# Encoder layer: two PSUM banks for attention's results and two for its scores, later v transposes, other homes, later sigmoids

## The chip, the cores and the metric

The kernel runs on one core of a Trainium2 chip. The core has a matrix engine, TensorE (PE), whose weight loads are listed apart (PEld); a vector engine, VectorE (DVE); a scalar engine, ScalarE (ACT); GpSimd (POOL); and SyncE (SP), which in this kernel issues nearly all transfers. Each engine takes its own instructions in order, and semaphores tie the engines together. PE writes into PSUM, which has eight banks of 128 x 512 float32 numbers; the other data lie in SBUF. The metric is the device time of one execution in microseconds (us), median of several. Lower is better.

## What is computed

One layer of an encoder on a sequence of 2048 tokens of width 1024, in float32:

```python
h = rms_norm(x, norm_mix[l])
z = h @ w_in[l]
q_a, k_a, v_a, q_b, k_b, v_b, g_a, g_b = jnp.split(z, offsets, axis=-1)
y_a = windowed_gqa(q_a, k_a, v_a, sink[l])           # 8 heads, 2 kv heads, |t-s| <= 128, ALiBi, sink
y_b = neighborhood_attn(q_b, k_b, v_b, rpb[l])       # 8 heads, 8 x 16 neighbourhood on a 32 x 64 grid
gates = jax.nn.sigmoid(jnp.concatenate([g_a, g_b], axis=-1) + b_gate[l])
merged = (gates[..., :D_MODEL] * (y_a @ w_proj_a[l])
          + gates[..., D_MODEL:] * (y_b @ w_proj_b[l]))
x = x + merged @ w_out[l]
h2 = rms_norm(x, norm_mlp[l])
x = x + jnp.square(jax.nn.relu(h2 @ w_up[l])) @ w_down[l]
return rms_norm(x, norm_final)
```

## The kernel before

Float32 products are made of three matmuls on split operands: each operand is cast to a high part (ACT) and the rest is kept as a low part (DVE or POOL), and high x high, high x low and low x high are added up in one PSUM bank (`mm3`, L202 to L205). One such triple over one of the eight slices of 128 features is called a plain step here; eight make a tile of 128 features by 512 tokens (`feature_steps`, L214).

The tokens are handled in four blocks of 512. An opening stage normalises `x` and makes `z` for blocks 0 and 1. Then comes the stretch that the change touches. In it PE does three things in turn: the plain steps of `z` for blocks 2 and 3 (the generator `fill`, a chain of tiles in the list `dense`), attention A (32 units: 2 kv heads by 16 query blocks, class `Unit`) and then attention B (32 units: 8 heads by 4 column groups, class `Near`). After it follow the gate stage (`gated`, L1474), the up and the down projection.

The order of PE in this stretch is written out by hand. `issued[0]` is the last PE instruction of the order, and `in_turn()` (L781) queues what is traced inside it behind that instruction. It binds only instructions on the same engine. All else (ACT, DVE, POOL, SP) is ordered by a scheduler, which places what its own simulation holds to be ready first, earlier lines of the program first.

A unit of A makes four scores (`score`, L801; matmuls L816): each takes an `s` bank, and DVE (L820) adds the bias, writes the sum to SBUF and takes the maximum. After the fourth, ACT makes the exponentials (L827) and POOL scales them (L831). Then, for each of up to three chunks of 128 keys, `turn` (L834) transposes the four parts into a `pt` bank (L838), ACT casts them to `ph` (L842), DVE makes `pl` (L843), and `product` (L846) multiplies them with the values into an `av` bank (L853, L854). After the last chunk ACT and DVE take the result out of that bank (L860, L861) and it is stored (`put`, and L176 a unit later). B does the same with four pairs of chunks to a unit (L1037 scores, L1044 DVE, L1052 exponentials, L1057 POOL, L1068 transposes, L1075 and L1076 parts, L1089 products, L1097 and L1098 result).

Scores of A run three units ahead of the products (`AHEAD`), those of B two units. The table `FIRST` (L907) says how many plain steps are given before certain scores of the first three units of A; scores before the first entry are not bound to the order. In the loops (L940, L1116) a turn is followed by scores of a later unit, then by plain steps up to a share of the whole (`plain`, L917), then by the product of the chunk before.

Tiles of v need a transpose by PE: `v_tile` (L728) copies the finished tile to SBUF (`A.copy(vt, ps)`, L737) and yields "turn"; the next call of `plain` then runs on to `v_parts` (L420), whose four transposes (L423) take another `mm` bank, and whose result ACT and DVE split (L436, L437) and SP stores (L741).

PSUM is shared out as `mm` 2 banks, `s` 3, `pt` 2, `av` 1 (L685). A request for a bank gets one that is free, and its first matmul waits for the readers of its old content.

SBUF is filled from two sides by pools (L691, L692 for A, L968, L969 for B). Pools of B lie where pools of A lay, so the first write to a tile of B waits for the last use of what lay there. Of the ones that matter, `qb2` (queries of every third unit of B) lies over the end of A's `pl`, `braw1` over the end of `ph`, and `biasl` (the wide biases, made by POOL from `braw` and `masks`, L994) over the rest of `ph` and the start of `pl`; `qb1` lies over `biasa1` and `byhead`. Units of B load their queries and make their bias in `load` (L1014; the loads are L988 and L1017).

At the end, `last_exp` (L1052) holds the last exponential of B, and the sigmoids of the gate stage (L1486) are queued behind it on ACT. The products of the second half of the gates take the three `s` banks (L1479).

Of the kernel before, what the change touches and what calls it, by code (L numbers as in the profile page):

```python
# [8 lines left out]
F32 = mybir.dt.float32  # L9
F32R = mybir.dt.float32r  # L10
# [12 lines left out]
P = 128  # L23
KC = D // P
NB = 4
BT = 512
# [69 lines left out]
def encoder_layer(ctx, tc, x, norm_mix, w_in, b_gate, sink, rpb, w_pa, w_pb, w_out,  # L96
# [112 lines left out]
        for _ in feature_steps(ps, hl, pages):  # L209
            pass  # L210

    issued = [None]

    def feature_steps(ps, hl, pages):  # L214

        hi, lo = pages
        for k in range(KC):
            issued[0] = mm3(ps, hl[:, 0, k, :], hl[:, 1, k, :], hi[k // 4][:, k % 4, :], lo[k // 4][:, k % 4, :],
                            k == 0, k == KC - 1)
            if k < KC - 1:  # L220
                yield "step"

# [459 lines left out]


    s_pp = ExitStack()
    pps.update({t: pool(f"pp_{t}", space=PSUM, stack=s_pp) for t in ("mm", "s", "pt", "av")})  # L685
    s_w = ExitStack()
    wp = pools(s_w, "right", ("raw", "whl", "z"), "w")
    s_h = ExitStack()
# [39 lines left out]
    def v_tile(col):  # L728
        raw = load_slice([(cols(w_in[0], col), KC)])
        yield  # L730
        hl = split_slice(raw, V if col == O_VA else G)
        yield
        for b in (2, 3):
            ps = psum("mm", 2)
            yield from feature_steps(ps, hl, hp[b])
            vt = T(wp, [P, 2, BT], F32, "z", 3)[:, 0]
            A.copy(vt, ps)  # L737
            yield "turn"
            out = v_parts(col, b, vt, psum("mm", 2), T(wp, [P, 2, BT], F32, "z", 3).rearrange("p a b -> p (a b)"))
            for dst, t in out:  # L740
                SY.dma_start(dst, t)  # L741
            yield


# [39 lines left out]
    class Unit:  # L784
# [16 lines left out]
        def score(self, u, forced=True):  # L801
            g, s = self.g, self.s
            if u == 0:
                if bias_a[g] is None:
                    with tc.issue_after(shares[2]):
                        make_bias_a(g)
                self.st = T(ap_, [P, 8, 4], F32, "sta", 8)
            mx, nm, sm, es, ri = (self.st[:, k, :] for k in range(5))
            sink_g = sink_p[:, g : g + 1]
            lo, hi = self.span[u]  # L810
            n = hi - lo
            base = (self.i - 1) * P
            ps = psum("s", 3)
            with in_turn() if forced else nullcontext():
                for z in range(2):
                    ins = PE.matmul(ps[:, :n], self.q[:, u].rearrange("p h q -> p (h q)"), kas[g][:, z, base + lo : base + hi],  # L816
                                    start=z == 0, stop=z == 1).ins
            if forced:
                issued[0] = ins
            V.tensor_tensor_reduce(out=s[:, u, lo:hi], in0=ps[:, :n], in1=bias_a[g][:, lo - u * A_Q : hi - u * A_Q],  # L820
                                   scale=1.0, scalar=sink_g, op0=ALU.add, op1=ALU.max, accum_out=mx[:, u : u + 1])
            if u < 3:
                return
            A.activation(nm, mx, AF.Copy, scale=-1.0)
            A.activation(es, mx, AF.Exp, bias=sink_g, scale=-1.0)
            for u, (lo, hi) in enumerate(self.span):
                A.activation(s[:, u, lo:hi], s[:, u, lo:hi], AF.Exp, bias=nm[:, u : u + 1], accum_out=sm[:, u : u + 1])  # L827
            V.tensor_tensor(out=sm, in0=sm, in1=es, op=ALU.add)
            V.reciprocal(ri, sm)
            for u, (lo, hi) in enumerate(self.span):  # L830
                share = G.tensor_scalar(s[:, u, lo:hi], s[:, u, lo:hi], ri[:, u : u + 1], 1.0, ALU.mult, ALU.mult)  # L831
            shares.append(share.ins)

        def turn(self, c):  # L834
            pt = psum("pt", 2)
            with in_turn():
                for u in range(4):
                    ins = PE.transpose(pt[:, u * P : (u + 1) * P], self.s[:, u, c * P : (c + 1) * P], ident).ins  # L838
            issued[0] = ins
            ph = T(ap_, [P, 512], F32R, "ph", 3)  # L840
            pl = T(ap_, [P, 512], F32R, "pl", 3)
            A.copy(ph, pt)  # L842
            V.tensor_tensor(out=pl, in0=pt, in1=ph.bitcast(F32), op=ALU.subtract)  # L843
            return ph, pl

        def product(self, c, ph, pl):  # L846
            g, i, c0, c1 = self.g, self.i, self.c0, self.c1
            v = vas[g]
            if c == c0:
                self.po = psum("av", 1)  # L850
            po = self.po
            with in_turn():
                PE.matmul(po, v[:, i - 1 + c, :], ph, start=c == c0, stop=False)  # L853
# [50 lines left out]
        load_kv(g, 0)  # L904
    units = [Unit(g, i) for g in (1, 0) for i in range(7)] + [Unit(g, i) for g in range(2) for i in range(7, 16)]
    AHEAD, PLAIN, SCORE, STEP = 3, 24 * KC, 0.27, 0.68
    FIRST = {(0, 3): 12, (1, 2): 14, (2, 0): 16, (2, 2): 18, (3, 0): 21}  # L907

    def prepare(n):
        if n + 2 < len(units):  # L910
# [1 line left out]
        if n + 1 < len(units):  # L912
            units[n + 1].order()

    given, owed = 0, [False]

    def plain(upto):  # L917
        nonlocal given
        while given < upto:
            if owed[0]:  # L920
                with in_turn():
                    next(fill)
            with in_turn():
                owed[0] = next(fill) == "turn"
            given += 1

    units[0].load()
# [2 lines left out]
    for n in range(AHEAD):  # L930
        prepare(n)
        for u in range(4):
            if (n, u) in FIRST:
                plain(FIRST[n, u])
            units[n].score(u, (n, u) >= (0, 3))
    plain(FIRST[AHEAD, 0])
    chunks = [(n, c) for n, x in enumerate(units) for c in range(x.c0, x.c1)]
    behind, scored, begin = [], 0, given
# [18 lines left out]
            y.product(*z)  # L957
    y, *z = behind.pop(0)
    y.product(*z)
    if owed[0]:  # L960
        next(fill)
        owed[0] = False
    flush(queue=SY)
    s_a.close()


    s_b = ExitStack()
    bp = pools(s_b, "right", ("masks", "kb0", "qb0", "braw0", "biass0", "stb", "biass1", "qb1", "qb2", "biasl", "braw1", "kb1"), "b")  # L968
    bp.update(pools(s_b, "left", ("sb0", "sb1", "sb2", "vb0", "vb1", "vb2", "phb", "plb", "yb"), "b"))  # L969
    boff, bstart, btotal = bias_layout()  # L970
    last_exp, last_parts, n_raw, n_short = [None], [None], [0], [0]
# [36 lines left out]
    class Near:  # L1008
# [17 lines left out]
        def score(self, i, forced=True):  # L1026
# [4 lines left out]
            kv = self.k.rearrange("p z (q f) -> p z q f", q=8)  # L1031
            s = self.s
            n = B_NR[i] * w
            ps = psum("s", 3)
            with in_turn() if forced else nullcontext():
                for z in range(2):
                    ins = PE.matmul(ps[:, :n], self.q[:, i, :],  # L1037
# [42 lines left out]
        def product(self, pair, ph, pl, pieces):  # L1080
            kp = 4 * self.w
            if pair == 0:
                self.po = psum("av", 1)
                pieces.reverse()
            po = self.po
            with in_turn():
# [29 lines left out]
    for at, (n, p) in enumerate(pairs):  # L1116
        x = units[n]
        if p == 0:
            if n % 4 == 2 and n + 6 < len(units):
                kbs[(n + 6) // 4] = load_k((n + 6) // 4)  # L1120
            if n + 3 < len(units):
                bias = units[n + 3].load(bias)
        if p == 1 and n + 2 < len(units):
            units[n + 2].load_v()
        behind.append((x, p, *x.turn(p)))
        if n + 2 < len(units):
            units[n + 2].score(p)
            scored += 1
        plain(begin + round(((at + 1) / len(pairs) * whole - scored * SCORE) / STEP))
        if len(behind) > 1:  # L1130
            y, *z = behind.pop(0)
            y.product(*z)
    y, *z = behind.pop(0)
    y.product(*z)
    flush(queue=SY)
    s_b.close()
    s_pg = ExitStack()
# [48 lines left out]
        def tile(self, *a, **k):  # L1186
            return psum("av", 1)

    wo = []

    def load_wo(n):
        rv = T(p4x, [P, D], F32, "xr", 5)
# [275 lines left out]
    for b in range(NB):  # L1468
# [5 lines left out]
        def gated(f, n):  # L1474
# [1 line left out]
            if n == 0:  # L1476
                hls[f] = slice_of([(cols(w_pa[0], f * P), 4), (cols(w_pb[0], f * P), 4)], V)
            hl = hls[f]
            ps = psum("mm" if n == 0 else "s", 2 if n == 0 else 3)  # L1479
            for c in range(4):  # L1480
                mm3(ps, hl[:, 0, 4 * n + c, :], hl[:, 1, 4 * n + c, :], yh[n][:, c], yl[n][:, c], c == 0, c == 3)
            if (b, f, n) not in loaded_gates:
# [284 lines left out]
```

## Time and profile before

| | us |
|---|---|
| median of 3 runs | 2614.03 (2612.89 to 2614.96) |
| the profiled execution | 2616.45 |
| its span, first to last instruction | 2614.0 |

The granted TensorE clock of the execution was 0.997 on the mean. Busy time by stage, in us, from the profile's windows:

| window | what runs | PE | DVE | ACT | POOL |
|---|---|---|---|---|---|
| 360 to 380 | first scores of A | 18.29 | 6.96 | 7.72 | 5.38 |
| 600 to 640 | end of A, start of B | 35.28 | 18.41 | 20.01 | 20.45 |
| 640 to 760 | B | 118.16 | 60.79 | 69.38 | 61.35 |
| 760 to 1020 | B | 256.40 | 112.24 | 143.42 | 119.43 |
| 1020 to 1040 | last plain steps | 20.00 | 7.09 | 8.53 | 0.00 |

How to read rows: in a timeline, a row is start, duration, engine, line of the kernel, operation, tiles out<-in, shape, count of merged instructions, and in brackets the idle time before it with the instruction or transfer that ended it. Matmuls overlap: a row's duration reaches into the next row. In the lists of waits a row is who waited for whom, microseconds in total, number of times, longest.

### The profile page before, as it was taken

The numbers are of one execution on the slowest core, as the hardware profiler recorded it, in microseconds if no ns is written. First come the engines' busy times: TensorE is split into PE (matmuls) and PEld (weight loads), VectorE is DVE, ScalarE is ACT, GpSimd is POOL, SyncE is SP. The second block draws the span as 40 slices with busy tenths as digits, with TensorE's granted clock in tenths as the row PEclk, the third lists the DMA queues.
The fourth block names the chain that finished last, engine by engine and source line by source line (L and its number), as shares of the span: only waits on it lengthen the run. The fifth ranks groups of instructions, "written<-read, shape, count | busy, mean of one in ns | idle before, by whom it ended". The sixth has DMA issues, their size and how long they took to land.

```text
span 2614.0 us, 34536 instructions
## 1 busy us (share of the span) xinstructions
PE 2571.5 (98%) x12140; PEld 2145.5 (82%) x12140; DVE 1608.9 (62%) x2621; ACT 1233.6 (47%) x2261; POOL 366.1 (14%) x493
## 2 busy tenths in 40 slices
PE   8999999999999999999999999999999999999999
PEld 6888878877888888888888888888888888888887
DVE  8866566665544443756578777766656535554766
ACT  5335356765555555533335544644444322322454
POOL 1000024444555541000001000100000000000010
PEclk9999999999999999999999999999999999999999
DMA  5657486566886746855556765854428835445555
GB/s 185 203 155 203 135 251 166 127 170 176 203 213 173 210 128 194 269 180 155 173 184 207 243 209 202 308 185 148 155 97 306 301 97 184 144 146 170 185 189 174
DMA packets 354125, 490.38 MB, mean 188 GB/s; under 512 B 28808, under 2 KB 188808, under 8 KB 351776
## 3 DMA queue, kind: packets, MB, share of 16 engines
q1 hardware_dynamic: 346896, 471.14, 58.3%
q10 hardware_dynamic: 7056, 17.04, 1.7%
q8 instruction: 95, 1.56, 0.3%
q14 instruction: 78, 0.64, 0.1%
HBM read 328.64 MB, written 159.45 MB: 187 GB/s over the span
## 4 chain that ended last, share of the span: by engine, by line
PE 90%; DMA 3%; DVE 3%; ACT 2%; issue 1%; SPq 1%; POOL 0%; POOLq 0%; DVEq 0%; ACTq 0%
PE b L311 15%; PE b L312 15%; PE b L313 15%; PE mm L203 5%; PE mm L205 5%; PE mm L204 5%; PE zb L311 3%; PE zb L313 3%; PE zb L312 3%; PE pt L203 2%; PE pt L204 2%; PE pt L205 2%; PE av L1089 2%; PE pt L1068 2%; PE s L1037 2%; PE pt L838 1%
## 5 line engine op out<-in xcount | busy, mean ns | idle before, releaser
L312 PE MATMUL b<-dwh,dah 128*128 128x512 f32 x896 | 348.5, 389 | 0.0
L313 PE MATMUL b<-dwh,dah 128*128 128x512 f32 x896 | 347.6, 389 | 0.0
L311 PE MATMUL b<-dwh,dah 128*128 128x512 f32 x896 | 339.6, 389 | 0.0
L307 ACT CAST dah<-da 128x1024 fp32r<-128x1024 f32 (+1 forms) x128 | 120.5, 942 | 369.2 <-PE b L313 245.3
L308 DVE TENSOR_TENSOR dah<-da,dah 128x1024 fp32r<-128x1024 f32 (+1 forms) x128 | 139.7, 1091 | 224.2 <-ACT dah L307 221.2
L312 PE MATMUL b<-ubh,uwhlb 128*128 128x512 f32 x592 | 230.4, 389 | 0.4 <-DVE ubh L308 0.4
L311 PE MATMUL b<-ubh,uwhlb 128*128 128x512 f32 x592 | 230.2, 389 | 0.0
L313 PE MATMUL b<-ubh,uwhlb 128*128 128x512 f32 x592 | 229.2, 389 | 0.0
L203 PE MATMUL mm<-hT,whl 128*128 128x512 f32 x544 | 219.5, 404 | 0.0
L205 PE MATMUL mm<-hT,whl 128*128 128x512 f32 x544 | 215.2, 396 | 0.0
L204 PE MATMUL mm<-hT,whl 128*128 128x512 f32 x544 | 214.6, 394 | 0.0
L313 PEld LDWEIGHTS b<-dwh,dah 128*128 128x128 f32 x896 | 168.2, 188 | 34.9
L311 PEld LDWEIGHTS b<-dwh,dah 128*128 128x128 f32 x896 | 168.2, 188 | 34.9
L312 PEld LDWEIGHTS b<-dwh,dah 128*128 128x128 f32 x896 | 168.2, 188 | 34.8
L311 PE MATMUL zb<-zh,zwhl 128*128 128x512 f32 x476 | 186.6, 394 | 6.6 <-DVE st L251 1.8
L312 PE MATMUL zb<-zh,zwhl 128*128 128x512 f32 x476 | 186.5, 392 | 0.0
L313 PE MATMUL zb<-zh,zwhl 128*128 128x512 f32 x476 | 183.6, 392 | 0.3 <-DVE zwhl L308 0.3
L302 DVE TENSOR_TENSOR uc<-b,uc 128x512 f32<-128x512 f32 x160 | 109.2, 689 | 104.1 <-PE b L313 103.1
L1637 POOL TENSOR_TENSOR st<-st,power 128x1 f32<-128x1 f32 x16 | 13.3, 841 | 925.2 <-DVE st L1636 925.2
L312 PEld LDWEIGHTS b<-ubh,uwhlb 128*128 128x128 f32 x592 | 111.2, 188 | 23.7 <-DVE ubh L308 0.8
L311 PEld LDWEIGHTS b<-ubh,uwhlb 128*128 128x128 f32 x592 | 111.1, 188 | 23.4 <-issue 0.4
L313 PEld LDWEIGHTS b<-ubh,uwhlb 128*128 128x128 f32 x592 | 111.1, 188 | 23.1
(255 smaller groups left out, 5847.4 us busy)
## 6 DMA issues: line engine op xcount, KB each, us to landing
at<-uc SPq DMA_DIRECT2D x224, 256.0 KB
da<-at SPq DMA_DIRECT2D x96, 512.0 KB
dw<-in_w_down_dram SPq DMA_DIRECT2D x160, 256.0 KB
uraw<-in_w_up_dram SPq DMA_DIRECT2D x32, 1024.0 KB
raw<-in_w_in_dram SPq DMA_DIRECT2D x34, 512.0 KB
zraw<-in_w_in_dram SPq DMA_DIRECT2D x16, 1024.0 KB
z<-zg SPq DMA_DIRECT2D x64, 256.0 KB
zg<-zc SPq DMA_DIRECT2D x32, 256.0 KB
```

The costliest lines, as they stand in the source:

```text
L203: PE.matmul(ps, lh, rh, start=first, stop=False)
L204: PE.matmul(ps, lh, rl, start=False, stop=False)
L205: return PE.matmul(ps, ll, rh, start=False, stop=last).ins
L302: return eng.tensor_tensor(out=out, in0=a, in1=b, op=op).ins
L307: casts.append(A.copy(hi, src).ins)
L308: return eng.tensor_tensor(out=lo, in0=src, in1=hi.bitcast(F32), op=ALU.subtract).ins
L311: PE.matmul(ps, lh, rh, start=first, stop=False, skip_group_check=True)
L312: PE.matmul(ps, lh, rl, start=False, stop=False, skip_group_check=True)
L313: PE.matmul(ps, ll, rh, start=False, stop=last, skip_group_check=True)
L1037: ins = PE.matmul(ps[:, :n], self.q[:, i, :], kv[:, z, B_R0[i] // 4 : (B_R0[i] + B_NR[i]) // 4, 4 * B_C0[j] : 4 * (B_C0[j] + w)], start=z ...
L1068: ins = PE.transpose(pt[:kp, at + (i - i0) * P : at + (i - i0 + 1) * P], self.s[i][:, rr : rr + kp], ident).ins
L1089: ins = PE.matmul(po[:, i0 * P : (i0 + ni) * P], self.v[:kp, c, :], src[:kp, o : o + ni * P], start=pair == x == z == 0, stop=(c == 7 and ...
```

## The change

It has six parts.

1. PSUM is shared out anew: `mm` 2, `s` 2, `pt` 2, `av` 1, `av1` 1. Units with odd numbers put their result into `av1`. In the gate stage every third product of the second half takes `av1` in place of an `s` bank.
2. The transposes of a v tile run after the fourth plain step of the next tile (`owed`), not directly behind the tile.
3. `FIRST` has other entries: scores are bound to the order from the third on, and 24 plain steps are given before the loop in place of 21. The total of steps stays.
4. The rings of `ph` and `pl` in A go from 3 to 2 buffers, and `braw1` changes places with `biasl`. With this `qb2` and `qb1` come to lie beyond everything of A, `braw1` over `biasa1` and `byhead`, and `biasl` over `ph` and `pl`.
5. The scores of B's third unit, which stood one behind each of the first unit's four turns, stand two and two behind its third and fourth turn.
6. `last_exp` is set to the last cast of `phb` (L1075), so that the sigmoids queue behind that.

```diff
-    issued = [None]
+    issued, owed = [None], []
...
             issued[0] = mm3(ps, hl[:, 0, k, :], hl[:, 1, k, :], hi[k // 4][:, k % 4, :], lo[k // 4][:, k % 4, :],
                             k == 0, k == KC - 1)
+            if k == 3 and owed:
+                owed.pop()()
...
-    pps.update({t: pool(f"pp_{t}", space=PSUM, stack=s_pp) for t in ("mm", "s", "pt", "av")})
+    pps.update({t: pool(f"pp_{t}", space=PSUM, stack=s_pp) for t in ("mm", "s", "pt", "av", "av1")})
...
             A.copy(vt, ps)
-            yield "turn"
-            out = v_parts(col, b, vt, psum("mm", 2), T(wp, [P, 2, BT], F32, "z", 3).rearrange("p a b -> p (a b)"))
-            for dst, t in out:
-                SY.dma_start(dst, t)
+
+            def finish(b=b, vt=vt):
+                out = v_parts(col, b, vt, psum("mm", 2), T(wp, [P, 2, BT], F32, "z", 3).rearrange("p a b -> p (a b)"))
+                for dst, t in out:
+                    SY.dma_start(dst, t)
+
+            owed.append(finish)
             yield
...
-            ps = psum("s", 3)
+            ps = psum("s", 2)
...
-            ph = T(ap_, [P, 512], F32R, "ph", 3)
-            pl = T(ap_, [P, 512], F32R, "pl", 3)
+            ph = T(ap_, [P, 512], F32R, "ph", 2)
+            pl = T(ap_, [P, 512], F32R, "pl", 2)
...
-                self.po = psum("av", 1)
+                self.po = psum("av1" if self.i % 2 else "av", 1)
...
-    FIRST = {(0, 3): 12, (1, 2): 14, (2, 0): 16, (2, 2): 18, (3, 0): 21}
+    FIRST = {(0, 2): 14, (1, 0): 16, (1, 2): 18, (2, 0): 20, (2, 2): 22, (3, 0): 24}
...
-    given, owed = 0, [False]
+    given = 0
...
         while given < upto:
-            if owed[0]:
-                with in_turn():
-                    next(fill)
             with in_turn():
-                owed[0] = next(fill) == "turn"
+                next(fill)
             given += 1
...
-            units[n].score(u, (n, u) >= (0, 3))
+            units[n].score(u, (n, u) >= (0, 2))
...
-    if owed[0]:
-        next(fill)
-        owed[0] = False
...
-    bp = pools(s_b, "right", ("masks", "kb0", "qb0", "braw0", "biass0", "stb", "biass1", "qb1", "qb2", "biasl", "braw1", "kb1"), "b")
+    bp = pools(s_b, "right", ("masks", "kb0", "qb0", "braw0", "biass0", "stb", "biass1", "qb1", "qb2", "braw1", "biasl", "kb1"), "b")
...
-            ps = psum("s", 3)
+            ps = psum("s", 2)
...
-                self.po = psum("av", 1)
+                self.po = psum("av1" if self.n % 2 else "av", 1)
...
         if n + 2 < len(units):
-            units[n + 2].score(p)
-            scored += 1
+            for i in ((p,) if n else ((), (), (0, 1), (2, 3))[p]):
+                units[n + 2].score(i)
+                scored += 1
...
     y.product(*z)
+    last_exp[0] = last_parts[0][0]
...
-    wo = []
+    wo, n_gate = [], [0]
...
-            ps = psum("mm" if n == 0 else "s", 2 if n == 0 else 3)
+            n_gate[0] += n
+            ps = psum("mm", 2) if n == 0 else psum("av1", 1) if n_gate[0] % 3 == 0 else psum("s", 2)
```

## The prediction

> **What bounds the kernel now.** I read the page first, then the waits of the matmul queue, then the timelines around the longest of them.
>
> ```profile
> span 2614.0 us, 34536 instructions
> PE 2571.5 (98%) x12140; PEld 2145.5 (82%) x12140; DVE 1608.9 (62%) x2621; ACT 1233.6 (47%) x2261; POOL 366.1 (14%) x493
> ```
>
> TensorE (PE) works 98% of the span. The change removes no matmul and adds none, so all it can win is time in which PE stands or runs slowly. The list of who kept PE waiting names the places; its columns are microseconds in total, number of waits, longest.
>
> ```profile
> PE mm L423 <- ACT z L737: 5.8, 5, 1.7
> PE av L853 <- DVE ya L861: 4.1, 6, 0.8
> PE s L1037 <- DMA qb<-qs_b: 4.0, 1, 4.0
> PE av L1089 <- DVE yb L1098: 3.5, 2, 3.2
> PE s L816 <- DVE sta L820: 1.7, 1, 1.7
> ```
>
> These five rows are what the five main edits aim at. They understate the loss: a wait is counted from the end of the matmul before, although in an undisturbed stream the next one starts before that end. The next part gives what each costs in start-to-start time.
>
> **The change part by part.** *Transposes of v tiles four steps later.* Now the four transposes (L423) stand directly behind the copy (L737) of the tile just finished.
>
> ```profile
> 617.32 0.40 PE L205 MATMUL mm<-hT,whl 128*128 128x512 f32 x1
> 618.39 0.66 PE L423 MATMUL mm<-ident,z 128*128 128x128 f32 x4 [0.68 <-ACT z L737]
> ...
> 564.82 1.36 SPq L741 DMA_DIRECT2D vs_b<-z  x2
> 584.88 0.61 SPq L1023 DMA_DIRECT2D vb<-vs_b  x1
> ...
> 627.60 0.39 PE L853 MATMUL av<-ph,va 128*128 128x512 f32 x1
> 627.83 0.39 PE L854 MATMUL av<-pl,va 128*128 128x512 f32 x1
> ```
>
> Undisturbed 512-column matmuls start 0.23 us apart (627.60 to 627.83). So L423 could have started at 617.55 and started at 618.39: 0.84 lost for a counted wait of 0.68, that is 0.16 more than the view counts. Five waits: 5.8 + 5 x 0.16 = 6.6 us. In the new order four plain steps (12 matmuls, 2.7 us) and the attention between them lie before the transposes, and the copy is over; I take the whole 6.6. If that cover were gone, 0.84 a time would return. What follows the transposes moves too: ACT and DVE split the result and SP stores it (L741), some 6 us later (four steps, each with a share of attention). Its reader (L1023) is issued 20 us after the last store of the first v tile of B, so that delay stays hidden. Of the two `mm` banks, the one given to the transposes was copied out four steps before; the next tile can take whichever comes free first. Bounds: 0 to 6.6.
>
> *Two banks for results.* The product of a new unit now waits until the last unit's result has left the only `av` bank.
>
> ```profile
> 421.52 0.39 PE L205 MATMUL mm<-hT,whl 128*128 128x512 f32 x1
> 422.74 0.50 PE L853 MATMUL av<-ph,va 128*128 128x512 f32 x1 [0.83 <-DVE ya L861]
> 423.07 0.39 PE L854 MATMUL av<-pl,va 128*128 128x512 f32 x1
> ...
> 380.00:600.00 220.00, 212.07 (x1191) 177.40 (x1190) 146.90 (x417) 152.70 (x429) 103.16 (x162) 1.00 0.58 154
> ```
>
> Here it costs 422.74 - 421.75 = 0.99, and L854 follows after 0.33 in place of 0.23. Six waits: 4.1 + 6 x 0.26 = 5.7 us in stage A. Units alternate between the two banks (two of 31 changes of unit in A fall on the same bank, where the order of work jumps), so I take 5.4. In the window from 380 to 600 (busy us: PE, weight loads, DVE, ACT, POOL) DVE has 146.9 of 220 and ACT 152.7, so they can follow a PE that comes a few per cent sooner. Bounds 0 and 5.7. Halving the rings of `ph` and `pl` from 3 to 2 costs nothing: a buffer's old reader, the product two chunks back, stands ahead of the new transposes in PE's own order.
>
> *Homes, and the third unit's scores two pairs later.* This is the largest single hole.
>
> ```profile
> 628.02 0.61 SPq L988 DMA_DIRECT2D braw<-tab  x1
> 628.74 0.56 SPq L1017 DMA_DIRECT2D qb<-qs_b  x1
> ...
> 628.49 0.49 PE L1068 MATMUL pt<-ident,sb 128*96 128x128 f32 x3
> 633.03 0.66 PE L1037 MATMUL s<-kb,qb 128*128 128x384 f32 x2 [4.05 <-DMA qb<-qs_b]
> 633.49 0.62 PE L203 MATMUL mm<-hT,whl 128*128 128x512 f32 x1
> ...
> 636.90 0.40 PE L205 MATMUL mm<-hT,whl 128*128 128x512 f32 x1
> ...
> 632.45 3.85 POOL L994 TENSOR_TENSOR biasl<-braw,masks 128x384 f32<-128x384 f32 x3 [1.15 <-DMA braw<-tab]
> ```
>
> The load of the queries (L1017) is issued only when stage A has read its last `pl` (L854 at 627.8), because `qb2` lies where `pl` lay and `braw1`, ahead of it in SP's queue, where `ph` lay. Three transposes take about 0.25, so PE loses 633.03 - 628.74 = 4.3 us. Then eight steps take 636.90 - 633.49 = 3.41 where 8 x 0.23 = 1.84 is usual: 1.6 more at a lowered clock. Together 5.9. With the smaller rings the homes of `qb2` and `braw1` fall above the end of `pl`, so both loads need not wait for it; `biasl` now lies over `ph` and `pl`, and its three additions (3.85 us on POOL) can start only about 628. The scores that need it come two pairs later, each pair with three plain steps (2 x 2.8 us): about 634, and the additions end about 632. I take 5.9; bounds 0 (the home doesn't help and the banks fill) to 5.9.
>
> *Sigmoids behind the last unit.* The wait of 3.2 us at the end of stage B is not a matter of banks.
>
> ```profile
> 997.15 0.39 PE L205 MATMUL mm<-hT,whl 128*128 128x512 f32 x1
> 1000.70 0.39 PE L1089 MATMUL av<-phb,vb 128*128 128x256 f32 x1 [3.16 <-DVE yb L1098]
> ...
> 1002.13 0.63 PE L205 MATMUL mm<-hT,whl 128*128 128x512 f32 x1
> ...
> 1005.12 0.41 PE L1089 MATMUL av<-phb,vb 128*128 128x256 f32 x1
> ...
> 993.67 1.28 ACT L1486 ACT_TABLE_LOAD   x1
> 994.97 2.56 ACT L1486 ACTIVATE z<-z,bg 128x512 f32<-128x512 f32 x4
> 997.43 0.46 ACT L1075 CAST phb<-pt 128x384 fp32r<-128x384 f32 x1
> ...
> 1032.35 0.62 ACT L1158 CAST page<-yraw 128x512 fp32r<-128x512 f32 x1 [3.68 <-DMA yraw<-y_b]
> ```
>
> ACT spends 1.28 + 2.56 = 3.84 us on a table and four sigmoids of the next stage, and the cast that attention needs comes behind them. PE loses 1000.70 - 997.38 = 3.3, then seven matmuls take 2.99 us where 1.6 is usual: 4.7 together. Short waits for the same bank (the view has one more, 0.3 + 0.16) add 0.5: 5.2 us in stage B. Moved behind the last `phb`, the 3.84 us meet an ACT that stands idle 3.68 us in one piece before 1032.35. Their reader is DVE in the gate stage, some 20 us on. I cost them at nothing; should the last page be late by all of it, 3.8 us. Bounds 1.4 to 5.2.
>
> *First scores.* Before, the fourth score waits for a bank, because DVE can start on the first only when the bias is there.
>
> ```profile
> 367.50 0.39 PE L205 MATMUL mm<-hT,whl 128*128 128x512 f32 x1
> 369.60 1.29 PE L816 MATMUL s<-ka,qa 128*128 128x256 f32 x6 [1.71 <-DVE sta L820]
> 370.69 0.63 PE L203 MATMUL mm<-hT,whl 128*128 128x512 f32 x1
> ...
> 373.25 1.06 PE L816 MATMUL s<-ka,qa 128*128 128x288 f32 x4
> ...
> 369.15 0.38 DVE L820 CUSTOM_DVE_ANT_0 sa<-s,biasa,byhead 128x160 f32<-128x160 f32 x1 [9.41 <-POOL biasa L758]
> ```
>
> PE loses 369.60 - 367.73 = 1.87, and six matmuls then take 2.56 us for a usual 1.4: 3.0 in all. After the change PE waits at the third score (two banks), but two steps later (+ 1.36) and with one score fewer ahead of it (- 0.25): it comes to it at about 368.8 and the bank is free at 369.6, so 0.8 us stays. Without a slow stretch the gain is 2.2; bounds 1.0 (the slow stretch stays) and 3.0.
>
> [...]
>
> *Two banks for scores.* This is the price. A score must now wait for DVE to have read the score two before it.
>
> ```profile
> 526.08 0.65 PE L816 MATMUL s<-ka,qa 128*128 128x192 f32 x4
> ...
> 525.67 0.44 DVE L820 CUSTOM_DVE_ANT_0 sa<-s,biasa,byhead 128x224 f32<-128x224 f32 x1
> ```
>
> The four instructions are two scores; the second starts near 526.36, and DVE ended the one two before at 526.11. That is the tightest place I found in A after the first scores: 0.25 us spare. In stage B the scores come one to a pair, some 2.1 us or more apart, so two banks are enough. I take 0.5 us; bounds 0 and 4 (a dozen tight places, 0.3 each). In the gate stage the two `s` banks and `av1` taken in turn are three banks as before: nothing.
>
> **Sum.** 6.6 + 5.4 + 5.9 + 5.2 + 2.2 - 0.5 = 24.8 us, say 25. The profiled execution took 2616.45 us (2614.0 of span and 2.45 around it) and becomes 2591.5; the median of the runs shown is 2.4 lower, 2614.03, and becomes **2589**.
>
> **The rivals.** *The next operand is late instead.* ACT is busy 69% of the window above and works in bursts; a product that no longer waits for its bank may wait for its `pl`, and the scores for DVE. Against it: of these I saw few in the trace, and two chunks lie between a cast and its product. Then stage A gives back its 5.4 and the 4 of the scores' upper bound: gain 16, **2598**.
>
> *The hole at the start of B stays*, since the additions to `biasl` still wait for the last product. For it: POOL adds for 3.85 us. Against it: the scores have been moved. Gain 25 - 5.9 = 19, **2595**.
>
> *The slow stretch at 370 stays*, because it has another cause than the wait before it. Against it: the slow steps begin where the wait ends. The gain is 24.8 - 1.2, near 24: **2590**. [...]
>
> *Slower: scores stall at every unit in stage A.* If the narrower ring lets DVE's queue order turn round, so that each of the 29 units scored inside the loop waits for its third and fourth score, the wait costs one DVE operation or two (0.4 to 0.5 each) with the time they queue. It decides from 25 / 29 = 0.86 us a unit; at 1.2 it costs 35 and the time is **2624**. Against it: the 0.25 spare at the tightest place.
>
> *The edits do not act*, because the order made for the other queues comes out differently and opens new waits of the same size: **2613**.
>
> **How the numbers follow.** Forecast 2589: 0.57. Slow stretch stays 0.08. Hole stays 0.10. Next operand late 0.14. No effect 0.05. Slower 0.06. About 0.2% (5 us) is what a measurement of this kernel can tell from no change. The first four are faster: 0.89; same 0.05; slower 0.06. The range goes down to the sum with every term at its best and the waits under the view's resolution gone too, 31 us: 2583, less 2 for other stages that fall differently; and up past the two partial rivals, 2600. The likeliest's own range is 2584 to 2594.
>
> **What would show it.** In the list of PE's waits the rows for L423, L853 on `ya`, L1037 on `qb` and L1089 on `yb` are gone or under 0.5 us each, and L816 on `sta` shows under 1 us near 369. The table load stands behind the last cast of `phb`. PE's first score of the third unit of B comes behind six plain steps. The gate stage starts 24 to 26 us earlier than now, and the stages behind it keep their length. The prediction is wrong if L816 waits on `sta` all through stage A, if L854 waits for `pl` in place of L853, or if a wait for a page or a weight opens at the start of the gate stage.

## The result, and the profile after

| kernel | median, us | range of runs | span of the profiled execution |
|---|---|---|---|
| before | 2614.49 | 2612.89 to 2616.09 | 2614.0 |
| changed | 2589.16 | 2587.67 to 2589.46 | 2587.6 |

The ratio is 0.9902, with a 95% interval of 0.9885 to 0.9919: 1.0% faster. The forecast was 2589, with a range of 2581 to 2600.

The two head lines of the page of the changed kernel:

```profile
span 2587.6 us, 34569 instructions
PE 2562.3 (99%) x12140; PEld 2142.1 (83%) x12140; DVE 1608.8 (62%) x2621; ACT 1234.9 (48%) x2261; POOL 366.9 (14%) x493
```

PE has as many instructions as before, and DVE, ACT and POOL are busy within 1.3 us of what they were. What is gone is time in which PE stood or ran slowly. Here are PE's waits in the changed kernel from 355 to 1060 us, the stretch that the change touches. In A the lines of the code are some five further down than before: L821 is the score (L816), L858 the product (L853), L866 the result on DVE (L861). In B they are one further up: L1036 is the score (L1037), L1067 the transposes (L1068), L1088 the product (L1089).

```profile
PE s L821 <- DVE sta L825: 1.1, 1, 1.1
PE av L858 <- DVE ya L866: 0.9, 1, 0.9
PE mm L203 <- DVE zc L304: 0.4, 1, 0.4
```

Three rows are left. The waits for the v tiles' copy, for the queries of B and for the result of B are gone altogether. In place of six waits for the bank of A's results there is one. No wait for an `s` bank stands in the loops; the row of L821 is the one at the first scores.

Where the time went can be read from three marks in PE's timeline: the first plain step of the stretch, the first turn of B and the first product of the gate stage. Before:

```profile
358.85 0.39 PE L203 MATMUL mm<-hT,whl 128*128 128x512 f32 x1
...
628.49 0.49 PE L1068 MATMUL pt<-ident,sb 128*96 128x128 f32 x3
...
1037.81 0.39 PE L203 MATMUL mm<-page,whl 128*128 128x512 f32 x1
```

Changed:

```profile
360.50 0.50 PE L203 MATMUL mm<-hT,whl 128*128 128x512 f32 x1 [0.39 <-DVE zc L304]
...
617.56 0.49 PE L1067 MATMUL pt<-ident,sb 128*96 128x128 f32 x3
...
1013.18 0.39 PE L203 MATMUL mm<-page,whl 128*128 128x512 f32 x1
```

From the first mark to the second it was 269.6 us and is 257.1: 12.6 less. From the second to the third it was 409.3 and is 395.6: 13.7 less. That is 26.3 us in the stretch, where 25 were forecast. The stretch began 1.65 us later than before, though no line ahead of it was changed; a second profile of the same changed kernel, below, has it at 358.33. From the third mark to the end this profile is 1.8 us shorter than the one of the kernel before, but the second profile of the changed kernel is 4.0 longer there than the first. So what happens ahead of the first mark and behind the third differs from one execution to the next, and I count only the stretch between them.

### The profile page after: what moved, and what is told of

It is laid out like the page before. It is cut to its first block, busy times and chain, and to the rows that moved or that the text cites. A ratio compares the mean times of both kernels' runs of the same rounds, so it can differ in the third digit from the quotient of the medians.

```text
span 2587.6 us, 34569 instructions
## 1 busy us (share of the span) xinstructions
PE 2562.3 (99%) x12140; PEld 2142.1 (83%) x12140; DVE 1608.8 (62%) x2621; ACT 1234.9 (48%) x2261; POOL 366.9 (14%) x493
## 4 chain that ended last, share of the span: by engine, by line
PE 94%; DVE 3%; DMA 2%; ACT 1%; issue 1%; SPq 0%; POOL 0%; POOLq 0%; DVEq 0%; ACTq 0%
PE b L313 16%; PE b L315 16%; PE b L314 16%; PE mm L205 6%; PE mm L203 6%; PE mm L204 6%; PE zb L313 3%; PE zb L315 3%; PE zb L314 3%; PE pt L203 2%; PE pt L204 2%; PE pt L205 2%; PE av L1088 2%; PE pt L1067 2%; PE s L1036 2%; PE pt L843 2%
```

## The experiments

All are the changed kernel with one part undone, unless the text says otherwise. The times are medians; the ratio to the kernel before stands beside them. Two measurements of the one changed program gave 2589.16 and 2588.19, with single runs from 2586.2 to 2591.6, so a difference of 2 us between two of these kernels says little by itself, and there the rows decide. A closer measure is the time from the first mark to the third in each run's profile: it is 652.7 us in one profile of the changed kernel and 652.9 in the other. It is one execution a run, so I read nothing into differences of half a microsecond. A table at the end of this section has it for all runs.

**Sigmoids behind the last exponential again.**

```diff
-    last_exp[0] = last_parts[0][0]
```

> The changed kernel with the sigmoids queued behind the last exponential again. My theory: the 3.84 us of table load and four sigmoids come between the exponentials of the last unit and its casts again, PE waits about 3.3 us near the end of B and then runs some 3 us at the lowered clock: 4.7 us more than the changed kernel, 2594. Rival: the second bank for results alone has absorbed that wait (it was put down to the bank): no such wait, 2589.

2590.68 us, ratio 0.991 (0.9896 to 0.9925). The sigmoids did go back between the exponentials and the casts. This is ACT's timeline in that run:

```profile
971.04 1.28 ACT L1487 ACT_TABLE_LOAD   x1
972.33 2.56 ACT L1487 ACTIVATE z<-z,bg 128x512 f32<-128x512 f32 x4
974.80 0.46 ACT L1074 CAST phb<-pt 128x384 fp32r<-128x384 f32 x1
```

And this is PE's:

```profile
974.52 0.39 PE L205 MATMUL mm<-hT,whl 128*128 128x512 f32 x1
975.31 0.39 PE L1088 MATMUL av<-phb,vb 128*128 128x256 f32 x1 [0.40 <-ACT phb L1074]
975.90 0.38 PE L1088 MATMUL av<-plb,vb 128*128 128x256 f32 x1 [0.21 <-DVE plb L1075]
```

A matmul of this kind starts 0.23 after the one ahead of it, so the product was due at 974.52 + 0.23 = 974.75. It comes 975.31 - 974.75 = 0.56 late for the cast and 0.47 more for the low part: 1.1 us with the restart, and no slow steps. The time behind the first turn of B bears it out: it is 396.9 us, against 395.6 and 396.1 in the changed kernel. My theory of 4.7 fell, and the rival was nearer. ACT is as late as it was; but the product now needs only its own operand. Before, it also needed the bank, and the copy out of the bank (L1097, then L1098 on DVE) stood behind table, sigmoids, cast, another copy and a weight split in ACT's queue. These are the rows of ACT and DVE in the kernel before, ahead of the product at 1000.70:

```profile
997.79 0.58 ACT L884 COPY z<-mm 128x512 f32<-128x512 f32 x1
998.27 1.05 ACT L179 CAST whl<-raw 128x1024 fp32r<-128x1024 f32 x1
999.34 0.58 ACT L1097 COPY yb<-av 64x512 f32<-64x512 f32 x1
...
999.95 0.69 DVE L1098 TENSOR_TENSOR yb<-av,yb 64x512 f32<-64x512 f32 x1 [1.47 <-DMA yraw<-y_b]
```

**One bank for results.**

```diff
-                self.po = psum("av1" if self.i % 2 else "av", 1)
+                self.po = psum("av", 1)
...
-                self.po = psum("av1" if self.n % 2 else "av", 1)
+                self.po = psum("av", 1)
```

> The changed kernel with all results of A and B in one bank, the scores still in two. My theory: the waits of the product for the last unit's result return, some 4.6 us in A and 1.4 us in B, six in all: 2595. Rival: these waits in the kernel before came from the other waits around them, and with those gone PE comes no earlier than the bank: under 2 us, 2590.

2596.79 us, ratio 0.9933 (0.9918 to 0.9948): 7.6 more than the changed kernel. By the marks it is 7.5, with 6.4 of it in A. PE's waits in the stretch:

```profile
PE av L858 <- DVE ya L866: 4.3, 8, 1.0
PE s L821 <- DVE sta L825: 0.8, 1, 0.8
PE av L1088 <- DVE yb L1097: 0.3, 1, 0.3
```

The waits in A are back, eight of them in place of the kernel before's six. In B, 0.3 is left and the long wait of 3.2 does not return: with the sigmoids out of the way one bank is enough there. Read with the run above, the long wait before needed both, the early sigmoids and the single bank, and either part of the change removes nearly all of it. The fourth case, early sigmoids and a single bank, is the kernel before, and also a run further down that has one other part of the change: both show 3.2.

**Transposes directly behind the tile again**, with the old `yield "turn"` and the old `plain`.

```diff
...
-            owed.append(finish)
+            yield "turn"
+            out = v_parts(col, b, vt, psum("mm", 2), T(wp, [P, 2, BT], F32, "z", 3).rearrange("p a b -> p (a b)"))
...
```

> The changed kernel with the transposes of a v tile directly behind the tile again. My theory: waits of PE for the copy return at half of the ten places, 6.6 to 7.4 us together: 2596. Rival: the place of the transposes matters only where PE had no other work between, and the fixed order now puts attention there: under 3 us, 2591.

2593.37 us, ratio 0.992 (0.9905 to 0.9935): 4.2 more, between the theory and the rival. PE's waits in the stretch:

```profile
PE mm L423 <- ACT z L737: 3.3, 4, 1.4
PE av L853 <- DVE ya L861: 0.9, 1, 0.9
PE pt L1068 <- POOL sb L1057: 0.5, 1, 0.5
PE s L816 <- DVE sta L820: 0.3, 1, 0.3
```

Four of the five waits come back, and they are shorter: 3.3 in place of 5.8. They stand at other tiles, too: two of them ahead of 400 us, where the kernel before has one, and none near 548 and 563, where it has 1.7 and 1.0. That the other edits have shifted what stands between a tile's last step and its transposes is the likely reason; I did not trace it tile by tile.

**The same part alone, put into the kernel before.**

> The kernel before with one part of the change alone, the transposes of v tiles after the fourth plain step of the next tile. My theory, since undoing this part in the changed kernel cost only 4.2 us: the seven us of such waits in the kernel before are all gone, but the kernel before gains only what its other waits leave, 5 to 7 us: 2608 to 2610. Rival: the place of these waits is taken by the one bank for results, and less than 4 us are gained: above 2610.5.

2611.4 us, ratio 0.9987 (0.9978 to 0.9997): 3.8 less than before. The row of L423 is gone, and PE's waits in the stretch read:

```profile
PE s L1036 <- DMA qb<-qs_b: 6.6, 1, 6.6
PE av L1088 <- DVE yb L1097: 3.5, 2, 3.2
PE av L858 <- DVE ya L866: 3.3, 5, 0.8
PE s L821 <- DVE sta L825: 2.0, 1, 2.0
PE mm L203 <- DVE zc L304: 1.7, 1, 1.7
PE av L859 <- DVE pl L848: 0.4, 2, 0.3
```

All of the 5.8 are saved, but another hole takes some back: the wait for the queries is 6.6 us where it was 4.0. By the marks the time up to the first turn of B is 7.3 us shorter than before (some of it because no slow steps follow the first scores here), and the time behind it 2.7 longer. That PE comes sooner to a fixed time is not why the hole grew: the load of the queries moves with the end of A, behind which it is issued, and here it took 6.2 us from its issue to the score in place of 4.3 (last section). The time is the rival's, but its reason is not: the waits for the bank of results have gone from 4.1 down to 3.3.

**Old homes, and the third unit's scores one behind each turn.**

```diff
-            ph = T(ap_, [P, 512], F32R, "ph", 2)
-            pl = T(ap_, [P, 512], F32R, "pl", 2)
+            ph = T(ap_, [P, 512], F32R, "ph", 3)
+            pl = T(ap_, [P, 512], F32R, "pl", 3)
...
-    bp = pools(s_b, "right", ("masks", "kb0", "qb0", "braw0", "biass0", "stb", "biass1", "qb1", "qb2", "braw1", "biasl", "kb1"), "b")
+    bp = pools(s_b, "right", ("masks", "kb0", "qb0", "braw0", "biass0", "stb", "biass1", "qb1", "qb2", "biasl", "braw1", "kb1"), "b")
...
-            for i in ((p,) if n else ((), (), (0, 1), (2, 3))[p]):
+            for i in (p,):
```

> The changed kernel with the old homes (three buffers of ph and pl in A, biasl ahead of braw1) and the third unit's scores of B one behind each turn from the first. My theory: the wait for the queries returns, 4.3 us and 1.6 us of lowered clock: 2595. Rival: the other edits have moved the end of A far enough for the load to come in time: under 2 us, 2590.

2597.05 us, ratio 0.9934 (0.9917 to 0.995): 7.9 more. PE's timeline in that run:

```profile
615.30 0.49 PE L1067 MATMUL pt<-ident,sb 128*96 128x128 f32 x3
622.39 1.01 PE L1036 MATMUL s<-kb,qb 128*128 128x384 f32 x2 [6.60 <-DMA qb<-qs_b]
623.20 0.63 PE L203 MATMUL mm<-hT,whl 128*128 128x512 f32 x1
...
627.04 0.88 PE L1067 MATMUL pt<-ident,sb 128*96 128x128 f32 x4
```

The hole is back and longer than before, 6.6 in place of 4.0, with nine matmuls at 0.43 us behind it. From the first turn to the score that waited it is 7.1 us; before it was 4.5.

**Each half of that by itself.** First the new homes with the scores one behind each turn:

> The changed kernel with its new homes, but the third unit's scores of B one behind each turn from the first. My theory: the new homes alone let the queries come early, so PE finds them; what can be late is the wide bias, which POOL makes only after the last product of A, and two banks hold back the third score for it by little: 0 to 1 us more than the changed kernel, 2589 to 2590. Rival: the bias fills both banks and PE waits 3 us or more at the third score: 2592 or above.

2590.4 us, ratio 0.9908 (0.9893 to 0.9922). PE's waits from 600 to 700 us are one row:

```profile
PE pt L1067 <- POOL sb L1056: 0.8, 1, 0.8
```

No wait for queries and none for the bias, so the rival fell. A wait of 0.5 for the same line of POOL, at nearly the same place, stands in the run with the transposes directly behind the tile, so I don't put this one down to the scores. Then the old homes with the scores two pairs later:

> The changed kernel with the old homes, but the third unit's scores of B two pairs later. My theory: two turns with their plain steps cover 5.6 us of the 6.8 us that PE waited with both parts undone, so a wait of 1 to 2 us stays: 2590 to 2591. Rival: the homes are the whole cure, because loads behind the blocked one in SP's queue are late too: 5 us or more, 2594.

2588.8 us, ratio 0.9903 (0.9888 to 0.9918). The same view:

```profile
PE s L1036 <- DMA qb<-qs_b: 0.7, 1, 0.7
```

The load is as late as before in SP's queue, and PE comes so late that 0.7 is left. Either half removes nearly all of the hole; the rival of the second half fell, and neither half's time can be told from that of the changed kernel.

**The old table of plain steps before the first scores.**

```diff
-    FIRST = {(0, 2): 14, (1, 0): 16, (1, 2): 18, (2, 0): 20, (2, 2): 22, (3, 0): 24}
+    FIRST = {(0, 3): 12, (1, 2): 14, (2, 0): 16, (2, 2): 18, (3, 0): 21}
...
-            units[n].score(u, (n, u) >= (0, 2))
+            units[n].score(u, (n, u) >= (0, 3))
```

> The changed kernel with the old table of plain steps before the first scores. My theory: PE reaches the bank that DVE has not yet read 1.4 us earlier, and waits that much longer, perhaps with some steps at the lowered clock: 1.5 to 3 us more, 2591 to 2592. Rival: the time is set by when the bias arrives, and PE makes the same work up later: no difference, 2589.

2590.56 us, ratio 0.9907 (0.9892 to 0.9922): 1.4 more, too little to be sure of by the time alone. PE's timeline:

```profile
369.43 2.42 PE L821 MATMUL s<-ka,qa 128*128 128x224 f32 x8 [1.73 <-DVE sta L825]
371.65 0.63 PE L203 MATMUL mm<-hT,whl 128*128 128x512 f32 x1
372.08 0.63 PE L204 MATMUL mm<-hT,whl 128*128 128x512 f32 x1
```

The wait is 1.7 again in place of 1.1, and steps of 0.43 us follow it. By the marks the run is 2.1 us longer than the changed kernel, in the range of my theory.

One wait beside another is not enough here, because the bias does not come at the same time in every execution: DVE's first addition of it (L825; L820 before) starts 10.0 to 11.4 us after the first mark, and the wait at the first scores follows that. With the new table and two banks for scores eight profiles have 0.3 to 1.65 us of wait, and in each the wait is that start less 9.7 to 9.9. With the old table, in the kernel before, in the run with the transposes alone and in this one, it is that start less 8.4 to 8.7. For a bias that comes at the same time the new table takes about 1.2 us off the wait, close to the 1.1 that was forecast.

**Three banks for scores and one for results.** It differs from the run with one bank for results only in the third `s` bank (which also takes the place of `av1` in the gate stage), and shows the price of taking that away.

> One bank for results and three for scores, all other parts as changed; to be read against the run with one bank for results and two for scores (2596.8), which differs only in the third bank for scores. My theory: two banks for scores cost next to nothing after the first scores, under 0.5 us, and near 1 us at them: 2596. Rival: the narrower ring costs a few tenths in each of a dozen units: 3 to 4 us less than that run, 2593.

2594.13 us, ratio 0.9926 (0.9909 to 0.9942), single runs from 2591.7 to 2599.1, against 2596.79. The times overlap. PE's waits:

```profile
PE av L858 <- DVE ya L866: 4.4, 8, 1.1
PE av L1088 <- DVE yb L1097: 0.3, 1, 0.3
```

The row of L821, 0.8 at the first scores, is all that the third bank takes away. In the loops two banks cost nothing that the list of waits shows. By the marks the third bank is worth 1.6 us, all of it ahead of the first turn of B. About 1.0 of that is the wait at the first scores from start to start, which leaves 0.6 for the loops: about the 0.5 of the forecast, as far as one profile each can tell, and not the rival's 3 to 4.

**One bank for scores**, the suspected price doubled; the gate stage then takes it and `av1` by turns.

```diff
-            ps = psum("s", 2)
+            ps = psum("s", 1)
...
-            ps = psum("mm", 2) if n == 0 else psum("av1", 1) if n_gate[0] % 3 == 0 else psum("s", 2)
+            ps = psum("mm", 2) if n == 0 else psum("av1", 1) if n_gate[0] % 2 == 0 else psum("s", 1)
```

> The suspected cost doubled: the changed kernel with one bank for scores in place of two (the gate stage then takes it and the second bank for results by turns). My theory: the spare time of scores in A is a few tenths with two banks, so with one bank each second score of a pair waits for DVE, about 1 us at 58 places, and in B nothing: 40 to 70 us more in A, 2640. Rival: DVE is quick enough behind PE that a pair loses 0.3 us: under 20 us, 2605.

2673.35 us, ratio 1.0226 (1.0211 to 1.0242): 84 more than the changed kernel, more than I had expected. PE's waits:

```profile
PE s L821 <- DVE sta L825: 54.6, 65, 1.8
PE pt L1067 <- POOL sb L1056: 5.4, 1, 5.4
PE s L1036 <- DVE stb L1043: 4.4, 5, 1.6
```

Sixty-five waits of 0.84 us on the mean, each with 0.16 that the view does not count, are some 65 us in A, and the other two rows have 10 more; some 7 of these stand where A goes over into B. The stretch is 82.6 us longer; some slow steps behind the wait of 5.4 make up 2 of what is missing, and the rest I did not follow up. From three banks to two costs 1.6 us; from two to one costs 3% of the kernel.

**The changed kernel once more.**

> The changed kernel once more, as the measure for the other runs of this call: 2589 within 2 us. Its profile shows how much the opening stage and the wait at the first scores differ between executions of one program: start of the plain steps between 358 and 360.5, wait at the first scores between 0.5 and 2 us.

2588.19 us, ratio 0.9901 (0.9886 to 0.9916). Its first plain step stands at 358.33 and its wait at the first scores is 0.8, so both move by about what was expected from one execution to the next.

**A version meant to be faster.** In the changed kernel A's units choose their bank by the number of the query block. Where the order jumps from block 15 of one kv head to block 7 of the other, both are odd and share `av1`; the wait of 0.9 stands at 553, where this jump falls. (At an earlier jump, from block 6 to block 0, both share `av`; no wait shows there.)

```diff
-                self.po = psum("av1" if self.i % 2 else "av", 1)
+                self.po = psum("av1" if self.at % 2 else "av", 1)
...
+    for at, x in enumerate(units):
+        x.at = at
...
-    FIRST = {(0, 2): 14, (1, 0): 16, (1, 2): 18, (2, 0): 20, (2, 2): 22, (3, 0): 24}
+    FIRST = {(0, 2): 16, (1, 0): 18, (1, 2): 20, (2, 0): 21, (2, 2): 23, (3, 0): 25}
```

> A version meant to beat the changed kernel: the two banks for results of A alternate by the order in which units run, so that the one place where two neighbours share a bank is gone, and two more plain steps are given before the third score. My theory: 1.1 us and 0.5 to 1.5 us less: 2587. Rival: the stretch after the first scores has less plain work to fill in and gives the second part back: 2588 or no difference.

2585.6 us, ratio 0.9893 (0.9879 to 0.9908), against 2588.19 and 0.9901 for the changed kernel on the same chip. The intervals overlap; the trace is clearer. The first two marks of its PE timeline:

```profile
358.93 0.39 PE L203 MATMUL mm<-hT,whl 128*128 128x512 f32 x1
...
613.13 0.49 PE L1069 MATMUL pt<-ident,sb 128*96 128x128 f32 x3
```

From mark to mark it takes 254.2 us, where the changed kernel took 257.1 and 256.8 in its two profiles, and its list of waits has no row of this stretch left. Both parts of it went in together, so what each is worth was not measured.

**All runs by the same marks.** The time from the first plain step of the stretch to the first turn of B, and from there to the first product of the gate stage, in us, one profile each; the last column is against the mean of the two profiles of the changed kernel:

| run | up to B | B and after | both | more than the changed kernel |
|---|---|---|---|---|
| changed | 257.1 | 395.6 | 652.7 | |
| changed, second profile | 256.8 | 396.1 | 652.9 | |
| sigmoids early | 256.2 | 396.9 | 653.1 | 0.4 |
| one bank for results | 263.3 | 396.9 | 660.3 | 7.5 |
| transposes directly behind | 259.4 | 397.0 | 656.5 | 3.7 |
| old homes, old places of scores | 256.5 | 405.2 | 661.7 | 8.9 |
| new homes, old places | 256.2 | 396.9 | 653.1 | 0.3 |
| old homes, new places | 257.4 | 396.6 | 654.0 | 1.2 |
| old table of steps | 259.3 | 395.6 | 654.8 | 2.1 |
| one bank for results, three for scores | 261.7 | 397.0 | 658.7 | 5.9 |
| one bank for scores | 334.5 | 401.0 | 735.4 | 82.6 |
| version meant to be faster | 254.2 | 395.6 | 649.8 | -3.0 |
| transposes alone in the kernel before | 262.4 | 412.1 | 674.4 | 21.7 |
| before | 269.6 | 409.3 | 679.0 | 26.2 |

## Why the prediction was right, step by step

| step | forecast, us | what the runs showed |
|---|---|---|
| v transposes | 6.6 | the row of 5.8 gone; alone in the kernel before 3.8 (by the marks 4.5), undone in the changed kernel 4.2 (3.7) |
| results, stage A | 5.4 | row of 4.1 down to 0.9; undone together with B's 7.6 (7.5) |
| homes and third unit | 5.9 | the hole gone; undone 7.9 (8.9); either half alone nearly enough |
| sigmoids and B's bank | 5.2 | the row of 3.5 gone; the sigmoids undone cost 1.5 (0.4), not told apart from nothing by the time |
| first scores | 2.2 | wait of 1.7 down to 1.1 and 0.8, no slow steps; the old table costs 1.4 (2.1) |
| two banks for scores | -0.5 | no wait in the loops; by the marks 1.6, of which 1.0 at the first scores |

*The sum.* PE's list of waits held the whole gain, and costing each row from start to start, with the slow steps behind it, gave 25 where the stretch shows 26.3. It holds by halves too. Four of the five waits for v tiles, the results of A, the first scores and the price of the banks stand up to the first turn of B: 11.8 us of the forecast, and 12.6 were gained there. The fifth wait for a v tile, the queries and the end of B stand behind it: 13.0 of the forecast, and 13.7 were gained. That PE's work was the same and the other engines had room was the ground of it, and that held. The terms do not hold one by one, though: undone one at a time they give 4.2, 7.6, 7.9, 1.5 and 1.4, 22.6 in all (3.7, 7.5, 8.9, 0.4 and 2.1 by the marks). Some waits had two causes, of which one is enough to cure them, and one hole grows when other waits are closed. The sum does not need the single prices, because all these waits go in the end. That the median came within 0.2 us of the forecast is luck: two measurements of the changed kernel lie 1.0 apart.

*The signs.* Two of the signs that the prediction named were missed by a little. The row of the product for `ya` was to be under 0.5 us and is 0.9, and that of the first scores was to be under 1 and is 1.1 in one of two profiles. The gate stage starts 24.6 us earlier, as said.

*The sigmoids.* One step failed: the sentence that the wait of 3.2 us "is not a matter of banks". The row itself named the bank's reader on DVE (L1098), and the runs with early sigmoids and with one bank show that it was a matter of both. The edit is right, but its price as the last one made is 1.1 us by the rows, not 4.7. Its other half held: behind the last cast, table and sigmoids run from 996.6 to 1000.3 on ACT, and no wait opens at the start of the gate stage.

*Results of A.* The forecast left a wait at the two jumps in the order of units. At one there is a wait, 0.9 us, and it is gone in the faster version, where the units alternate at the jumps too. The term was sized from the waits before, six of them; with PE earlier there would be eight, as the run with one bank shows, and that run is 6.4 us longer in A, so the bank is worth more than 5.4 once the rest is done.

*Homes and scores.* Both were costed as one term, and either alone does nearly all of it. That `biasl` could be late was the doubt. In the changed kernel POOL adds for it from 617.8 to 621.7, and PE makes the first score of that unit at 623.7, so 2 us are to spare, as in the forecast. With the scores left at their old places and the new homes, no wait for it appears.

*First scores.* The forecast of 0.8 us left was met by 1.1 and 0.8, and the bias decides which it is. That the slow stretch goes with the wait was taken from the row alone, where steps of 0.43 us follow a wait of 1.71. With the old table both came back together, and in both profiles of the changed kernel the wait is short and the slow steps are gone. But the row was read too widely: the kernel before has two more waits of that length, for v tiles, without slow steps. This is the first of them:

```profile
547.77 0.66 PE L423 MATMUL mm<-ident,z 128*128 128x128 f32 x4 [1.74 <-ACT z L737]
...
548.49 0.39 PE L204 MATMUL mm<-hT,whl 128*128 128x512 f32 x1
548.72 0.39 PE L205 MATMUL mm<-hT,whl 128*128 128x512 f32 x1
```

The granted clock was 1.00 from 547.8 to 551, and 0.67 from 369 to 374, at the first scores. (Behind the two long waits of the kernel before it was 0.57 from 633 to 637 and 0.71 from 1000.7 to 1004.) So a wait of 1.7 us can be followed by slow steps and need not be, and that none stood in the changed kernel's profiles was not sure beforehand (last section).

*The rivals.* That the next operand is late instead did not happen: no row for `pl` is left, where 0.4 stood before (of the changed kernel's variants only that with the old table of steps has 0.4 again). That scores stall at every unit did not happen with two banks; with one it does, in 65 places. The price I gave it, 1.2 us a unit, would have been too low there.

## What to carry to other kernels

Where one engine is the bound, read each wait from start to start, look at what runs slowly behind it, and ask of each whether it has one cause or two: a late operand and a busy buffer together make a long wait of which either cure takes most (here 3.2 us, of which 0.6 or 0.3 was left). Do not add up cures measured alone, since a hole further on can grow and give part of them back (here one of 4.0 us to 6.6). Where medians lie too close, compare the same stretch between two marks in the profiles. A ring can be narrowed for next to nothing as long as its reader is done before the writer returns; find that spare time in the timeline first, because one buffer further on can lie a cliff (here 1.6 us from three to two, 84 us from two to one).

## What I had not expected of the hardware

Waits of nearly the same length were followed by slow steps at one place in two programs (1.71 us in the kernel before, 1.73 with the old table of steps), and by none at other places and in other programs. The row of 1.73 us above, with the old table of steps, has them. This one, from the run with the old homes, has not:

```profile
370.17 0.84 PE L821 MATMUL s<-ka,qa 128*128 128x224 f32 x4 [1.65 <-DVE sta L825]
370.84 0.39 PE L203 MATMUL mm<-hT,whl 128*128 128x512 f32 x1
371.07 0.40 PE L204 MATMUL mm<-hT,whl 128*128 128x512 f32 x1
```

Its steps are 0.23 apart. So are those behind the wait of 2.0 in the run with the transposes alone, while each of the six waits of 3.2 to 6.6 us that stand in this stretch in all traces together is followed by seven or more slow matmuls. So among waits of 1.65 to 2.0 us the length alone does not decide; what else does was not tried.

The load of the queries did not always take the same time. From its issue to the score that waited for it it is 4.3 us in the kernel before (628.74 to 633.03), and 6.2 in the three other runs in which a score waited for it: with homes and scores undone, with the homes alone undone, and with the transposes alone. With homes and scores undone it was issued at 616.15 and used at 622.39. That is 1.9 of the 2.5 us by which the hole was longer in that run than before; the rest is that the load was issued 0.85 us after the first turn in place of 0.25. In all three runs with 6.2 a load of weights (`raw`, 512 KB) was issued 2.4 us behind that of the queries, and the core's transfers moved 1.65 to 1.68 MB in that time, at 261 to 267 GB/s. In the kernel before the next such load was issued at 635.36, after the score, and 0.81 MB were moved at 184 GB/s. That the two loads held each other up fits this; no run moved the load of weights alone, so it is not shown.
